# Shifted buffers for the quarters of h, an adding DMA for one branch's low parts, and six raw weight buffers in a three-branch mixer layer

## The chip, the cores and the metric

The kernel runs on one core of one Trainium2 chip. The metric is the device time of one execution in microseconds; of several runs the median is given. TensorE does the matmuls, VectorE (DVE in the rows) and ScalarE (ACT) prepare their operands and finish their results, GpSimd (POOL) does small work, and SyncE (SP) issues the loads. PEld is TensorE's loading of the stationary operand, which overlaps the matmuls.

## The reference, cut to what matters

x has 512 tokens of 1,024 channels, all in float32. One layer is computed:

```python
h = rmsnorm(x, norm_g)
proj = h @ w_in                       # 1024 x 12288
a_u, a_v, a_z, b_p, b_z, c_h, c_b, c_c, c_z, gate_logits = split(proj)
ya = spatial_gating(gelu(a_u), gelu(a_v), ...) * silu(a_z)
yb = multiscale_pool(b_p, pool_w, pool_b, pool_scale) * silu(b_z)
yc = c_b * causal_depthwise_conv(c_c * c_h, conv_w, conv_b) * silu(c_z)
gates = sigmoid(gate_logits)          # three of 1024 channels
merged = gates[0]*(ya @ w_branch_a) + gates[1]*(yb @ w_branch_b) + gates[2]*(yc @ w_branch_c)
out = rmsnorm(x + merged @ w_out)
```

## The kernel before

Each float32 operand of a matmul is split into a high part (rounded to the format that TensorE reads, `F32R`) and a low part (what is left). A product of two operands is then three matmuls: high by high, high by low and low by high (`mm3`, lines 97 to 101). The high part of a weight is a cast on ScalarE and the low part a subtraction on VectorE (`split`, lines 51 to 54).

A weight goes through three pools. `load_raw` (lines 56 to 59) fetches it into one of seven `wraw` buffers of 4 KB per partition, on SP's queue. `load_w` (lines 61 to 66) splits it into one of four `whi` and one of four `wlo` buffers. A buffer is used again as soon as its last reader is through, so SP's queue waits for raw buffers, and ScalarE's casts wait for TensorE to release high parts.

The projections of h are computed in 22 groups of 512 output channels (`group`). A group takes four quarters of its weight, combines them by sums, and makes seven products of 128x256 matmuls (line 435) in place of eight, each with 24 matmuls. h, transposed, is kept as quarters (`b11`, `b21`, `b22`) and as sums of quarters (`t1` to `t4`), each with a high and a low part: 14 buffers of 4 KB per partition from the pool `forms`, made by `form_tile` (lines 170 to 172) under the tags f0 to f6. The seven products stream b11, b21, t2, t1, t3, b22 and t4 in this order. Later the same tags hold the split merged result and the residual.

The branches follow each other: a, b, c. In each, `merge` computes the sigmoid gates in two groups and multiplies the branch's result by its weight: `cols` loads 256 columns in two units of 512 KB with `load_w`, `proj` makes a tile of 128 output channels from 24 matmuls of 512 columns, and `under` multiplies it by the gate and adds it to `merged`. One pair of units serves two tiles. Branch b has four such pairs, two in each half: the first tile of a half is computed by `mix` ahead of the rest of the pending group (b22, t4), the others in `after`. Branch b's pooling, ahead of it, is work for VectorE.

The order of the instructions on each engine is set when the program is built: a planner takes them by their place in the program and by when its own costs say that inputs and buffers are there. Only what stands in `pin` keeps the order of the program (the start, mainly). The same planner deals out buffers and the waits for them.

Of the kernel before, what the change touches and what calls it, by code (L numbers as in the profile page):

```python
# [8 lines left out]
F32 = mybir.dt.float32  # L9
F32R = mybir.dt.float32r  # L10
AF = mybir.ActivationFunctionType
ALU = mybir.AluOpType
PSUM = bass.MemoryType.PSUM

P = 128
# [3 lines left out]
NB = S // P  # L19
HALF = 512  # L20
GC = 256
RMS_EPS = 1e-6
LN_EPS = 1e-5
POOL_WINDOWS = (2, 4, 8, 16)
# [6 lines left out]
def mixers_kernel(ctx, tc, x, norm_g, w_in, sgu_ln_g, sgu_ln_b, sgu_w, sgu_b, pool_w, pool_b, pool_scale,  # L31
                  conv_w, conv_b, w_branch_a, w_branch_b, w_branch_c, w_out, final_g, out):
    nc = tc.nc
# [1 line left out]
    const = ctx.enter_context(tc.tile_pool(name="const", bufs=1))  # L35
    acts = ctx.enter_context(tc.tile_pool(name="acts", bufs=1))
    forms = ctx.enter_context(tc.tile_pool(name="forms", bufs=1))
    wraw = ctx.enter_context(tc.tile_pool(name="wraw", bufs=7))
    wsum = ctx.enter_context(tc.tile_pool(name="wsum", bufs=2))
    whi = ctx.enter_context(tc.tile_pool(name="whi", bufs=4))  # L40
    wlo = ctx.enter_context(tc.tile_pool(name="wlo", bufs=4))
# [9 lines left out]
    def split(hi, lo, src, keep=lambda ins: ins):  # L51

        keep(nc.scalar.copy(out=hi, in_=src))  # L53
        keep(nc.vector.tensor_tensor(out=lo, in0=src, in1=hi.bitcast(F32), op=ALU.subtract))  # L54

    def load_raw(src, shape):
        raw = wraw.tile([P, *shape], F32, tag="wraw", name="wraw")
        nc.sync.dma_start(out=raw, in_=src)
        return raw

    def load_w(src, shape, keep=lambda ins: ins):
        raw = load_raw(src, shape)
        hi = whi.tile([P, *shape], F32R, tag="whi", name="whi")
        lo = wlo.tile([P, *shape], F32R, tag="wlo", name="wlo")
        split(hi, lo, raw, keep)
        return hi, lo

    def cols(w2d, c0):

        v = w2d[:, c0 : c0 + GC].rearrange("(k p) c -> p k c", p=P)  # L70
        units = [load_w(v[:, 4 * h : 4 * h + 4, :], [4, GC]) for h in range(2)]

        def at(k, j):
            hi, lo = units[k // 4]
            return hi[:, k % 4, j * P : (j + 1) * P], lo[:, k % 4, j * P : (j + 1) * P]

        return at

    def halves(w2d, c0, keep=lambda ins: ins, homes=None):

        v = w2d[:, c0 : c0 + HALF].rearrange("(k p) c -> p k c", p=P)
        units = []
        for h in range(4):
            src = v[:, 2 * h : 2 * h + 2, :]
            if homes is None:
                units.append(load_w(src, [2, HALF], keep=keep))
            else:
                split(*homes[h], load_raw(src, [2, HALF]), keep)
                units.append(homes[h])

        def at(k):
            hi, lo = units[k // 2]
            return hi[:, k % 2, :], lo[:, k % 2, :]

        return at
# [73 lines left out]

    def form_tile(name, tag):  # L170

        return tuple(forms.tile([P, 4, GC], F32R, tag=f"{tag}{e}", name=f"{name}{e}") for e in ("h", "l"))


    hq = {(0, 0): form_tile("b11", "f0"), (1, 0): form_tile("b21", "f1"), (1, 1): form_tile("b22", "f2"),
          (0, 1): form_tile("b12", "f6")}

    def h_at(e, k, b):
# [5 lines left out]
    def x_rstd(b, parts=1):  # L184
        n = D // parts
        ms = RMS_EPS
        for i in range(parts):
# [140 lines left out]

    hsum = acts.tile([P, 4, 4, GC], F32, tag="ylo", name="hsum")
    for i, q in enumerate([(0, 0), (0, 1), (1, 1), (1, 0)]):  # L330
# [4 lines left out]
    def sum_form(name, tag, out, in0, in1):  # L335
        nc.vector.tensor_tensor(out=out, in0=in0, in1=in1, op=ALU.subtract)
        moving[name] = form_tile(name, tag)
        split(*moving[name], out)
# [29 lines left out]
    for b in range(NB):  # L368
        v_tile(w, b, 1)
        if b == 0:  # L370
            sbias = const.tile([P, KT, P], F32, tag="pad1", name="sbias")
            for h in range(2):
                ps = bank()
                nc.tensor.matmul(ps, lhsT=ones, rhs=wsT[:, 4 * h : 4 * h + 4, :], start=True, stop=True)
                for g in range(4):
                    t = 4 * h + g
# [20 lines left out]
    def proj(w, j, rhs_hi, rhs_lo, nk=KT):  # L397
        ps = bank()
        for k in range(nk):
            mm3(ps, w(k, j), (rhs_hi[:, k, :], rhs_lo[:, k, :]), k == 0, k == nk - 1)  # L400
        return ps

    def tile512(name):
        return tmp.tile([P, PAD + S], F32, tag="tmp", name=name)[:, 0:S]

    def out_tile(name):

        return outs.tile([P, 2, 2, S], F32, tag="outs", name=name)
# [5 lines left out]

    T1, T2 = slice(0, GC), slice(GC, S)

# [3 lines left out]
    def group(c0, g, ct, use=None):  # L420
        def quarter(kh, nh):
            c = c0 + nh * HALF + g * GC
            return load_raw(w_in[kh * HALF : (kh + 1) * HALF, c : c + GC].rearrange("(k p) c -> p k c", p=P), [4, GC])
# [88 lines left out]
    def act_into(ct, func):  # L512
        def use(src, half, ts):
            nc.scalar.activation(out=ct[:, half, :, ts], in_=src, func=func)
        return use
# [52 lines left out]
    def merge(br, w_branch):  # L568

        state = {}  # L570

        def gates(g):
            state[g] = out_tile("gate")
            yield from group(OFF[f"g{br}"], g, state[g], act_into(state[g], AF.Sigmoid))

        def split_m(ts):
            hi, lo = m_split[ts.start // 2]
            split(hi, lo, merged[:, ts, :])

        def mixes(g):  # L580
            wb = {}

            def mix(t):
                if t % 2 == 0:
                    wb[t // 2] = cols(w_branch, t * P)
                return proj(wb[t // 2], t % 2, y_hi, y_lo)

            def under(t, ps):
                nonlocal merged
                if merged is None:  # L590
                    merged = acts.tile([P, KT, S], F32, tag="big", name="merged")
                gate = state[g][:, t // 4, t % 2]
                if br == 0:
                    nc.vector.tensor_mul(out=merged[:, t, :], in0=ps, in1=gate)
                    return
                pr = tile512("pr")
                nc.vector.tensor_mul(out=pr, in0=ps, in1=gate)
                nc.vector.tensor_add(out=merged[:, t, :], in0=merged[:, t, :], in1=pr)
                if br == 2 and g == 1 and t % 2 == 1:
                    if not m_split:  # L600
                        for kk in range(4):
                            m_split[kk] = tuple(
                                forms.tile([P, 2, S], F32R, tag=f"f{kk}{e}", name=f"m_{e}") for e in ("h", "l"))
                        split_m(slice(0, 2))
                        split_m(slice(4, 6))
                    split_m(slice(t - 1, t + 1))

            first = mix(TILES[g][0])

            def after():  # L610
                under(TILES[g][0], first)
                for t in TILES[g][1:]:
                    under(t, mix(t))

            return after

        for g in range(2):
            items.append(("group", gates(g), None))
            items.append(("other", lambda g=g: mixes(g)))
# [52 lines left out]
    def pool_mm(p):  # L672
        hi, lo = load_w(pool_w[0, p].rearrange("(k p) c -> p k c", p=P), [2, GC])
        w = lambda k, j: (hi[:, k, j * P : (j + 1) * P], lo[:, k, j * P : (j + 1) * P])
        ts = slice(2 * p, 2 * p + 2)
        pss = [proj(w, j, y_hi[:, ts, :], y_lo[:, ts, :], nk=2) for j in range(2)]

        def after():
            for j, ps in enumerate(pss):
                t = 2 * p + j  # L680
                y = tile512("y")
                nc.vector.scalar_tensor_tensor(out=y, in0=ps, scalar=vec(2, t), in1=silu_z[p % 2][:, p // 2, j],  # L682
                                               op0=ALU.add, op1=ALU.mult)
                nc.scalar.mul(out=y_hi[:, t, :], in_=y, mul=vec(3, t))
                nc.vector.scalar_tensor_tensor(out=y_lo[:, t, :], in0=y, scalar=vec(3, t),  # L685
                                               in1=y_hi[:, t, :].bitcast(F32), op0=ALU.mult, op1=ALU.subtract)

        return after
# [75 lines left out]
    for c in range(2):  # L764
        w = halves(w_out, c * HALF)
        cs = slice(c * HALF, (c + 1) * HALF)
        for b in range(NB):
# [9 lines left out]
            if c == 0:  # L777
                nc.vector.tensor_scalar(out=ms0[:, b : b + 1], in0=ssq, scalar1=1.0 / D, scalar2=RMS_EPS,
                                        op0=ALU.mult, op1=ALU.add)
# [38 lines left out]
```

## Time and profile before

| | |
|---|---|
| median of 3 runs | 714.74 us (714.09 to 715.19) |
| the profiled execution | 714.31 us |
| its span in the profile | 712.1 us |
| TensorE's mean granted clock in it | 0.994 |
| read from HBM | 73.96 MB |

The profile shows one execution, in us from the start of its span. A row of the timeline has the start, the duration, the engine (SPq is SyncE's queue), the line, the operation, what it writes and reads, and in brackets how long the engine stood idle before and what ended that. A matmul's shown duration is longer than its step to the next one, since they overlap. L54 is line 54 of the kernel.

### The profile page before, as it was taken

To read this page: it belongs to the slowest core of one execution; us is meant where nothing else is said; L and a number is where in the kernel's file an instruction comes from. 1 tells how busy PE (TensorE), PEld (TensorE's weight loads), DVE (VectorE), ACT (ScalarE), POOL (GpSimd) and SP (SyncE) were. 2 spreads that over 40 slices of the span, in tenths; PEclk is the share of its full clock that TensorE was granted. 3 is DMA by queue.
4 is the path that set the end of the run, shared out by engine and by line. 5 is a ranking of instruction groups with operands and counts; after the bars stand their busy time and mean duration, and the time that the engine had idled before them with its cause. 6 is when DMAs were issued, how large, how long until landed. Compare 5 with 4: busy or idle time off the path is not lost.

```text
span 712.1 us, 11488 instructions
## 1 busy us (share of the span) xinstructions
PE 697.6 (98%) x4838; PEld 650.7 (91%) x4838; DVE 539.2 (76%) x620; ACT 334.6 (47%) x410; POOL 15.0 (2%) x38
## 2 busy tenths in 40 slices
PE   8999999999999999997999999999999999999996
PEld 6779999999898999996989899999999999898884
DVE  6998789795545799999665777798979986646453
ACT  6534556555233456455434334545545464244232
POOL 3001000000000000000000000000000000000001
PEclk9999999999999999999999999999999999999998
DMA  7822323314141313340514213224332334172002
GB/s 281 260 82 60 114 65 119 119 53 157 58 148 60 114 50 106 117 147 2 179 60 151 86 60 120 89 92 138 97 119 93 117 119 144 63 260 95 1 26 93
DMA packets 68536, 76.81 MB, mean 108 GB/s; under 512 B 2492, under 2 KB 61956, under 8 KB 68484
## 3 DMA queue, kind: packets, MB, share of 16 engines
q1 hardware_dynamic: 67892, 75.02, 32.5%
q10 hardware_dynamic: 592, 1.05, 0.4%
q8 instruction: 38, 0.62, 0.4%
q14 instruction: 14, 0.11, 0.1%
HBM read 73.96 MB, written 2.10 MB: 107 GB/s over the span
## 4 chain that ended last, share of the span: by engine, by line
PE 90%; DVE 6%; DMA 1%; issue 1%; ACT 1%; SPq 0%; POOL 0%; POOLq 0%; ACTq 0%; DVEq 0%
PE ps L435 58%; PE ps L99 9%; PE ps L100 9%; PE ps L101 9%; PE ps L259 2%; DVE wlo L54 1%; DMA x_in<-in_x 1%; PE ps L553 1%; DVE win L658 1%; DVE ylo L685 0%; DVE wraw L448 0%; DVE y L682 0%; ACT whi L53 0%; DVE d L661 0%; DVE ylo L54 0%
## 5 line engine op out<-in xcount | busy, mean ns | idle before, releaser
L53 ACT CAST whi<-wraw 128x1024 fp32r<-128x1024 f32 (+1 forms) x168 | 174.5, 1040 | 275.5 <-PE ps L435 171.0
L54 DVE TENSOR_TENSOR wlo<-wraw,whi 128x1024 fp32r<-128x1024 f32 (+1 forms) x168 | 201.6, 1208 | 84.5 <-ACT whi L53 84.1
L99 PE MATMUL ps<-yhi,whi 128*128 128x512 f32 x208 | 81.1, 390 | 0.0
L100 PE MATMUL ps<-ylo,whi 128*128 128x512 f32 x208 | 81.1, 390 | 0.0
L101 PE MATMUL ps<-yhi,wlo 128*128 128x512 f32 x208 | 80.9, 389 | 0.0
L435 PE MATMUL ps<-b21h,wlo 128*128 128x256 f32 x176 | 50.6, 287 | 3.9 <-DVE wlo L54 3.9
L448 DVE TENSOR_TENSOR wraw<-wraw 128x1024 f32<-128x1024 f32 x44 | 53.6, 1219 | 0.4
L435 PE MATMUL ps<-b22h,whi 128*128 128x256 f32 x176 | 51.1, 290 | 0.0
L435 PE MATMUL ps<-b21h,whi 128*128 128x256 f32 x176 | 50.3, 286 | 0.0
L435 PE MATMUL ps<-t1h,whi 128*128 128x256 f32 x176 | 49.9, 284 | 0.4 <-ACT whi L53 0.4
L435 PE MATMUL ps<-b21l,whi 128*128 128x256 f32 x176 | 50.3, 286 | 0.0
L435 PE MATMUL ps<-t2h,whi 128*128 128x256 f32 x176 | 50.1, 285 | 0.0
L435 PE MATMUL ps<-t2h,wlo 128*128 128x256 f32 x176 | 50.0, 284 | 0.0
L435 PE MATMUL ps<-b11h,wlo 128*128 128x256 f32 x176 | 49.9, 284 | 0.1
L435 PE MATMUL ps<-t1h,wlo 128*128 128x256 f32 x176 | 49.8, 283 | 0.0
L435 PE MATMUL ps<-t3h,whi 128*128 128x256 f32 x176 | 49.8, 283 | 0.0
L435 PE MATMUL ps<-t3l,whi 128*128 128x256 f32 x176 | 49.8, 283 | 0.0
L435 PE MATMUL ps<-t3h,wlo 128*128 128x256 f32 x176 | 49.8, 283 | 0.0
L435 PE MATMUL ps<-t4h,wlo 128*128 128x256 f32 x176 | 49.8, 283 | 0.0
L435 PE MATMUL ps<-t4l,whi 128*128 128x256 f32 x176 | 49.8, 283 | 0.0
L435 PE MATMUL ps<-b11l,whi 128*128 128x256 f32 x176 | 49.8, 283 | 0.0
L435 PE MATMUL ps<-t1l,whi 128*128 128x256 f32 x176 | 49.8, 283 | 0.0
(221 smaller groups left out, 1830.6 us busy)
## 6 DMA issues: line engine op xcount, KB each, us to landing
wraw<-in_w_in SPq DMA_DIRECT2D x96, 512.0 KB, 3.7
wraw<-in_w_branch_a SPq DMA_DIRECT2D x8, 512.0 KB
wraw<-in_w_branch_b SPq DMA_DIRECT2D x8, 512.0 KB, 3.5
wraw<-in_w_branch_c SPq DMA_DIRECT2D x8, 512.0 KB, 4.0
wraw<-in_w_out SPq DMA_DIRECT2D x8, 512.0 KB
res<-in_x SPq DMA_DIRECT2D x4, 512.0 KB, 4.9
x_in<-in_x SPq DMA_DIRECT2D x3, 512.0 KB, 10.1
wraw<-in_pool_w SPq DMA_DIRECT2D x4, 256.0 KB, 2.6
```

The costliest lines, as they stand in the source:

```text
L53: keep(nc.scalar.copy(out=hi, in_=src))
L54: keep(nc.vector.tensor_tensor(out=lo, in0=src, in1=hi.bitcast(F32), op=ALU.subtract))
L99: nc.tensor.matmul(ps, lhsT=a[0], rhs=b[0], start=first, stop=False)
L100: nc.tensor.matmul(ps, lhsT=a[0], rhs=b[1], start=False, stop=False)
L101: nc.tensor.matmul(ps, lhsT=a[1], rhs=b[0], start=False, stop=last)
L259: pin(nc.tensor.matmul(vps[b], lhsT=a, rhs=r, start=done[b] == 1, stop=done[b] == 3 * KT))
L435: nc.tensor.matmul(ps[:, j * GC : (j + 1) * GC], lhsT=a[x][:, k, j * P : (j + 1) * P], rhs=moving[b][y][:, k, :], start=first and j == 0 a ...
L448: nc.vector.tensor_tensor(out=out, in0=in0, in1=in1, op=op)
L553: nc.tensor.matmul(mx[:, n * P : (n + 1) * P], lhsT=v_t[:, n, t * P : (t + 1) * P], rhs=wsT[:, t, :], start=True, stop=True)
L658: nc.vector.tensor_add(out=nxt[:, lo:], in0=cur[:, lo:], in1=cur[:, lo - step : PAD + S - step])
```

## The change

The 14 buffers of `form_tile` get a few more elements each, and the data begin `SHIFT[tag + e]` elements of 4 bytes into them, a number that differs between the tags. In branch b (`br == 1`) `load_w` makes the low part in another way: ScalarE copies the raw weight to the high part and writes the negated high part into the low buffer, and a DMA on GpSimd's queue adds the weight from HBM to it. The pool of raw weights has six buffers in place of seven, and the DMA scratch is 2,048 bytes in place of 1,024.

```diff
--- before.py
+++ after.py
@@ -19,6 +19,9 @@
 NB = S // P
 HALF = 512
 GC = 256
+
+SHIFT = {"f0h": 64, "f0l": 64, "f1h": 0, "f1l": 64, "f5h": 112, "f5l": 112, "f3h": 120, "f3l": 56,
+         "f4h": 32, "f4l": 32, "f2h": 16, "f2l": 16, "f6h": 8, "f6l": 8}
 RMS_EPS = 1e-6
 LN_EPS = 1e-5
 POOL_WINDOWS = (2, 4, 8, 16)
@@ -35,7 +38,7 @@
     const = ctx.enter_context(tc.tile_pool(name="const", bufs=1))
     acts = ctx.enter_context(tc.tile_pool(name="acts", bufs=1))
     forms = ctx.enter_context(tc.tile_pool(name="forms", bufs=1))
-    wraw = ctx.enter_context(tc.tile_pool(name="wraw", bufs=7))
+    wraw = ctx.enter_context(tc.tile_pool(name="wraw", bufs=6))
     wsum = ctx.enter_context(tc.tile_pool(name="wsum", bufs=2))
     whi = ctx.enter_context(tc.tile_pool(name="whi", bufs=4))
     wlo = ctx.enter_context(tc.tile_pool(name="wlo", bufs=4))
@@ -62,8 +65,15 @@
         raw = load_raw(src, shape)
         hi = whi.tile([P, *shape], F32R, tag="whi", name="whi")
         lo = wlo.tile([P, *shape], F32R, tag="wlo", name="wlo")
-        split(hi, lo, raw, keep)
+        if by_dma:
+            nc.scalar.copy(out=hi, in_=raw)
+            nc.scalar.mul(out=lo, in_=hi.bitcast(F32), mul=-1.0)
+            nc.gpsimd.dma_start(out=lo, in_=src, accum_op=ALU.add)
+        else:
+            split(hi, lo, raw, keep)
         return hi, lo
+
+    by_dma = False
 
     def cols(w2d, c0):
 
@@ -169,7 +179,12 @@
 
     def form_tile(name, tag):
 
-        return tuple(forms.tile([P, 4, GC], F32R, tag=f"{tag}{e}", name=f"{name}{e}") for e in ("h", "l"))
+        parts = []
+        for e in ("h", "l"):
+            at = SHIFT[tag + e]
+            t = forms.tile([P, 4 * GC + at], F32R, tag=f"{tag}{e}", name=f"{name}{e}")
+            parts.append(t[:, at:].rearrange("p (k t) -> p k t", k=4))
+        return tuple(parts)
 
 
     hq = {(0, 0): form_tile("b11", "f0"), (1, 0): form_tile("b21", "f1"), (1, 1): form_tile("b22", "f2"),
@@ -605,13 +620,19 @@
                         split_m(slice(4, 6))
                     split_m(slice(t - 1, t + 1))
 
+            nonlocal by_dma
+            by_dma = br == 1
             first = mix(TILES[g][0])
 
             def after():
                 under(TILES[g][0], first)
+                nonlocal by_dma
                 for t in TILES[g][1:]:
+                    by_dma = br == 1
                     under(t, mix(t))
-
+                by_dma = False
+
+            by_dma = False
             return after
 
         for g in range(2):
@@ -801,7 +822,7 @@
     import concourse.bacc as bacc
     from concourse.bass_utils import run_bass_kernel_spmd
 
-    nc = bacc.Bacc("TRN2", target_bir_lowering=False, num_devices=1, dynamic_dma_scratch_size=1024)
+    nc = bacc.Bacc("TRN2", target_bir_lowering=False, num_devices=1, dynamic_dma_scratch_size=2048)
     arrays, args = {}, {}
     for name in _INS:
         a = np.ascontiguousarray(inputs[name])
```

## Rows read from the trace of the kernel before

**Rows 1.** The page, first part: busy time and its share of the span.
```profile
PE 697.6 (98%) x4838; PEld 650.7 (91%) x4838; DVE 539.2 (76%) x620; ACT 334.6 (47%) x410; POOL 15.0 (2%) x38
```

**Rows 2.** Windows: length; busy us of PE, PEld, DVE, ACT, POOL; granted clock; DMA.
```profile
300.00:328.00 28.00, 27.95 (x210) 26.65 (x209) 27.97 (x47) 16.05 (x24) 0.00 (x0) 1.00 0.36 114
328.40:332.20 3.80, 0.00 (x0) 0.00 (x0) 3.54 (x6) 1.91 (x3) 0.00 (x0) 0.94 0.00 0
331.80:335.10 3.30, 2.88 (x13) 2.88 (x14) 3.27 (x4) 0.05 (x1) 0.00 (x0) 0.50 0.00 0
345.90:420.00 74.10, 74.10 (x449) 66.53 (x448) 46.27 (x49) 27.86 (x31) 0.00 (x0) 1.00 0.31 98
```

**Rows 3.** Timeline of VectorE and TensorE at the hole.
```profile
330.95 1.22 DVE L54 TENSOR_TENSOR wlo<-wraw,whi 128x1024 fp32r<-128x1024 f32 x1
...
332.22 0.58 PE L435 MATMUL ps<-b21h,wlo 128*128 128x256 f32 x1 [3.88 <-DVE wlo L54]
```

**Rows 4.** Timeline of TensorE, a product of 256-column matmuls.
```profile
421.44 0.28 PE L435 MATMUL ps<-t2h,wlo 128*128 128x256 f32 x1
421.56 0.28 PE L435 MATMUL ps<-t2h,whi 128*128 128x256 f32 x1
```

**Rows 5.** Timeline of ScalarE: the casts of the eight units of w_branch_b.
```profile
338.10 1.05 ACT L53 CAST whi<-wraw 128x1024 fp32r<-128x1024 f32 x1
340.48 1.05 ACT L53 CAST whi<-wraw 128x1024 fp32r<-128x1024 f32 x1 [1.32 <-PE ps L435]
...
354.38 1.05 ACT L53 CAST whi<-wraw 128x1024 fp32r<-128x1024 f32 x1 [4.81 <-PE ps L435]
...
357.26 1.05 ACT L53 CAST whi<-wraw 128x1024 fp32r<-128x1024 f32 x1 [0.87 <-ACT gate L514]
...
379.31 1.05 ACT L53 CAST whi<-wraw 128x1024 fp32r<-128x1024 f32 x1 [1.29 <-PE ps L435]
382.19 1.05 ACT L53 CAST whi<-wraw 128x1024 fp32r<-128x1024 f32 x1 [1.83 <-PE ps L435]
...
396.34 1.05 ACT L53 CAST whi<-wraw 128x1024 fp32r<-128x1024 f32 x1 [4.81 <-PE ps L435]
...
399.22 1.05 ACT L53 CAST whi<-wraw 128x1024 fp32r<-128x1024 f32 x1 [0.87 <-ACT gate L514]
```

**Rows 6.** Timeline of TensorE: first matmuls that read those units' low parts.
```profile
346.38 0.39 PE L101 MATMUL ps<-yhi,wlo 128*128 128x512 f32 x1
...
349.12 0.39 PE L101 MATMUL ps<-yhi,wlo 128*128 128x512 f32 x1
...
363.06 0.39 PE L101 MATMUL ps<-yhi,wlo 128*128 128x512 f32 x1
...
388.34 0.39 PE L101 MATMUL ps<-yhi,wlo 128*128 128x512 f32 x1
...
405.02 0.39 PE L101 MATMUL ps<-yhi,wlo 128*128 128x512 f32 x1
```

**Rows 7.** The page, DMA: a queue (packets, MB, share); issues (size, us to landing).
```profile
q1 hardware_dynamic: 67892, 75.02, 32.5%
...
wraw<-in_w_in SPq DMA_DIRECT2D x96, 512.0 KB, 3.7
...
wraw<-in_w_branch_b SPq DMA_DIRECT2D x8, 512.0 KB, 3.5
...
x_in<-in_x SPq DMA_DIRECT2D x3, 512.0 KB, 10.1
```

**Rows 8.** Timeline of SyncE, VectorE and ScalarE in the steady stretch of branch c.
```profile
415.08 0.37 SPq L58 DMA_DIRECT2D wraw<-in_w_in  x1
...
421.24 0.37 SPq L58 DMA_DIRECT2D wraw<-in_w_in  x1
...
418.85 1.22 DVE L448 TENSOR_TENSOR s<-wraw 128x1024 f32<-128x1024 f32 x1 [0.65 <-DMA wraw<-in_w_in]
...
432.84 1.05 ACT L53 CAST whi<-wraw 128x1024 fp32r<-128x1024 f32 x1 [1.39 <-issue]
```

## The prediction

> **What bounds the kernel now.** I read the page's busy times first: TensorE is busy for 98% of the span and VectorE for 76% [rows 1]. The reader should see that little but matmul time can be won. The windows come next, over the one stretch where TensorE stands still [rows 2]: from 300 to 328 us VectorE is busy for all but 0.03 us of 28, then TensorE does nothing for the 3.8 us from 328.4, and its granted clock is 0.50, the 1.2 GHz level, for the 3.3 us after 331.8. The timeline names the cause [rows 3]: the low part of a weight was made on VectorE only at 330.95, and the matmul behind it waited 3.88 us. Elsewhere matmuls follow each other at a fixed step: 0.12 us at 256 columns [rows 4]. At 2.4 GHz 256 columns are 0.107 us, so some 13 ns of each step are not columns. So the kernel is bound by TensorE, with one hole of about 5.5 us (3.8 idle, and half of the 3.3 us at 1.2 GHz, 1.7) that VectorE makes.
>
> **Part 1, the offsets.** They add no instruction and no byte. The 14 buffers start at other addresses, all shifts multiples of 32 bytes (8 elements of 4). What could change is the step of the 22 x 7 x 24 = 3,696 matmuls that stream these buffers. The kernel before has all 14 at the same place modulo 4 KB, so no row shows another place. Upper bound of the gain: all 13 ns go, 3,696 x 13 = 48 us. Bound of the loss, from the same row mirrored: 13 ns more, +48 us. I take zero: within a quarter the four slices and the two weight halves start 1,024 and 512 bytes apart, and the step is 0.12 us from one to the next all the same [rows 4].
>
> **Part 2, the adding DMA.** In branch b alone (8 of the 132 loads of weights), the subtraction on VectorE goes, and a negated copy on ScalarE and a second fetch of the weight by a DMA that adds come in its place. Removed: 8 x 1.22 us on VectorE [rows 3]. They stand at 340 us and later, behind the hole [rows 2], so by themselves they can't fill it. Added: 8 negations on ScalarE, each like the cast, 1.05 us [rows 5]; ScalarE has gaps of 0.87 to 4.81 us beside those casts, so they fit. Added on GpSimd: 8 DMA issues, which wait for the negation; GpSimd has nothing else until the last stage (no busy time in the windows [rows 2]), so nobody is queued behind them there. Added on the DMA engines: 8 x 512 KB.
>
> What counts is the time from the end of the negation to the first matmul that reads the low part, the third one of each tile (line 101). There are four pairs of loads. First of each pair: the casts end at 339.15, 355.43, 380.36 and 397.39 us; with 1.05 for the negation the DMA can start at 340.20, 356.48, 381.41 and 398.44 [rows 5]. The matmuls that need it start at 346.38, 363.06, 388.34 and 405.02 [rows 6]. Slack: 6.2, 6.6, 6.9 and 6.6 us. Second of each pair: starts at 342.58, 359.36, 384.29 and 401.32, needed 2.74 us (twelve matmuls) after the first [rows 6]; slack 6.5, 6.4, 6.8 and 6.4 us. The slack is about the same each time because a buffer for the high part only comes free when TensorE has finished with the product four places earlier.
>
> The DMA itself is in no row. From below: a plain load of these bytes from this tensor lands 3.5 us after its issue, 3.7 for w_in. From above: the early loads of x, which stood behind others, took 10.1 [rows 7]. An adding DMA has to read the destination as well as the source; as two loads one after the other, that is 2 x 3.7 = 7.4 us. I take 7.4, which lies near the middle. The first units are then late by 1.2, 0.8, 0.5 and 0.8, together 3.3 us. The second ones share the engines with the first: 75.02 MB took 32.5% of the 16 engines' 712 us [rows 7], so 512 KB take 1.6 us of all of them and with two reads 3.2 us. The second starts 2.4 us after the first in pair one and 2.9 in the others, so it loses another 0.8 and three times 0.3 us. Its waits, after the first one's wait has moved TensorE, are 0.5, 0.5, 0.4 and 0.5, together 1.9. Sum of part 2: 5.2 us. All of it is on the path: behind a waiting matmul stands every later one. Gaps of about 1 us are far below the 3.8 us that stood before the slow clock [rows 2], so I add nothing for the clock.
>
> The Trainium skill speaks for less. Its page "DMA: Bandwidth & Descriptors" (Anatomy of one DMA, the GpSimd path) gives 2.0 us plus the bytes over 436 GB/s, which for 512 KB is an estimate of 3.2 us. "Collectives: The Full Stack" (The bandwidth ceiling) says that an add in the DMA costs two source reads and not the adding itself. By both together the DMA would take about 4.4 us, no matmul would wait, and the sum would be zero. No run here shows either yet.
>
> **Part 3, six raw buffers instead of seven.** Each load waits for one more release on SP's queue. In a group of the steady stretch, the load issued at 415.08 would go out at the next release, 421.24, and land 3.7 us later, at 424.9; the sum on VectorE that now starts at 418.85 waits for it [rows 8]. After it come two more operations of 1.22 us, so the operand is ready at 428.6. The cast that reads it runs at 432.84 [rows 8], for a product still further off: 4.2 us of margin, cost zero. If VectorE's order were kept as it is, other low parts would stand behind that late sum; their lead is about two products of 24 x 0.12 = 2.9 us, against a delay of 6.1, so 0.3 to 0.4 us a group and, over the 20 groups that follow another, at most 8 us. The order is the planner's, made anew with six buffers, so I keep zero and leave the 8 to the range. From below nothing: fewer buffers release nothing sooner. SP's queue holds only loads there.
>
> **Sum.** The profiled execution took 714.31 us; with 5.2 it is 719.5. That execution was 0.43 under the median of the runs shown, so the forecast is 719.9.
>
> **Rivals.** *Hidden* (0.22): the DMA lands within 6.2 us, and nothing waits: 714.7 us. For it: the plain load's 3.7 leaves 2.5 us for the second read. Against: another queue, and each pair overlaps on the engines. The two pages of the Trainium skill above speak for this case.
>
> *A slow queue* (0.17): either the DMA takes the upper bound of 10.1 us, the first units wait 3.9, 3.5, 3.2 and 3.5 and the second ones some 2 in all, +16, 731 us; or the second DMA starts only when the first has landed. Then the second lands 14.8 us after the first could start, 4.7 us late, each pair loses 5.5, and the gaps are long enough for the slow clock (1.7 each) [rows 2]: 4 x 7.2 = 29, 743 us. Nothing in this trace shows that queue at work.
>
> *The hole closes* (0.14), the other side: with six buffers and eight fewer operations the planner orders VectorE's work anew, and the late low part [rows 3] no longer stands behind the others. It decides if that subtraction starts before 328 instead of at 330.95. Price: the 5.5 us of the hole, 709.2, if the DMA is hidden too. Against: the removed operations come later than the hole, and VectorE's work ahead of it is all still there.
>
> *The offsets matter* (0.10), also faster: two reads on the way to TensorE that now start at the same place modulo 4 KB stop disturbing each other. It decides once the step of any of the seven products falls below 0.12 us; half of the 13 ns would be 24 us, 691. Against it: the even step at every slice [rows 4].
>
> **How the numbers follow.** The forecast has 0.37. About 0.2% (1.4 us) is what a measurement of this kernel can tell from no change. Faster: 0.14 + 0.10 = 0.24. Within it: 0.22. Slower: 0.37 + 0.17 = 0.54. The range goes from 709, the closed hole, to 733, just above the DMA's upper bound; it leaves out the offsets' 0.10 and about half of the slow queue, 0.08, and holds the 8 us of part 3. A loss from the offsets has no chance of its own: no row hints at one.
>
> **What would show it.** Right: matmuls of line 101 in the four tiles that open a pair with a wait of about 1 us that ends on a DMA; GpSimd's queue with 8 issues and a landing of 7 to 8 us; 4 MB more read; the step at 0.12 us in all seven products; the hole near 328 us as before. Wrong: a landing under 6 us with no wait (hidden), one DMA starting only when the last has ended (slow queue), a step under 0.12 us in some product (offsets), or no hole (planner).

## The result and the profile after

The changed kernel takes 743.97 us (741.88 to 745.72), the kernel before 714.70 in the runs beside it: the ratio is 1.0409, with a 95% interval of 1.0376 to 1.0441. The change costs 29.3 us.

The page of the kernel after, its busy times (they answer to [rows 1]), its DMA queues and issues (to [rows 7]) and the costliest group with a new wait. The last number of an issue's line is the median time from the issue to the landing, when all the data are there:

```profile
PE 705.6 (95%) x4838; PEld 651.4 (88%) x4838; DVE 530.1 (72%) x612; ACT 342.6 (46%) x418; POOL 25.7 (3%) x46
...
q1 hardware_dynamic: 67892, 75.02, 31.5%
q0 software_dynamic: 4224, 4.19, 3.7%
...
L111 PE MATMUL ps<-yhi,wlo 128*128 128x512 f32 x208 | 85.7, 412 | 18.4 <-DMA wlo<-in_w_branch_b 18.4
...
wlo<-in_w_branch_b POOLq DMA_DIRECT2D x8, 512.0 KB, 6.9
```

VectorE has 9.1 us less to do and TensorE as many matmuls as before, but the third matmul of `mm3` (line 101 before, 111 now) stands idle for 18.4 us, all of it behind the adding DMA. GpSimd's timeline in the kernel after shows the first four of its eight issues:

```profile
340.44 1.45 POOL L71 DMA_DIRECT2D wlo<-in_w_branch_b  x1 [194.75 <-PE ps L450]
350.93 1.32 POOL L71 DMA_DIRECT2D wlo<-in_w_branch_b  x1 [9.04 <-issue]
365.25 1.29 POOL L71 DMA_DIRECT2D wlo<-in_w_branch_b  x1 [13.00 <-ACT wlo L70]
373.15 1.31 POOL L71 DMA_DIRECT2D wlo<-in_w_branch_b  x1 [6.61 <-DVE wlo L57]
```

TensorE's timeline in the kernel after shows the eight waits, in brackets:

```profile
350.71 0.79 PE L111 MATMUL ps<-yhi,wlo 128*128 128x512 f32 x1 [4.42 <-DMA wlo<-in_w_branch_b]
356.60 0.50 PE L111 MATMUL ps<-yhi,wlo 128*128 128x512 f32 x1 [0.40 <-DMA wlo<-in_w_branch_b]
372.88 0.50 PE L111 MATMUL ps<-yhi,wlo 128*128 128x512 f32 x1 [2.15 <-DMA wlo<-in_w_branch_b]
378.92 0.50 PE L111 MATMUL ps<-yhi,wlo 128*128 128x512 f32 x1 [1.42 <-DMA wlo<-in_w_branch_b]
404.11 0.79 PE L111 MATMUL ps<-yhi,wlo 128*128 128x512 f32 x1 [2.49 <-DMA wlo<-in_w_branch_b]
410.61 0.57 PE L111 MATMUL ps<-yhi,wlo 128*128 128x512 f32 x1 [1.92 <-DMA wlo<-in_w_branch_b]
428.80 0.50 PE L111 MATMUL ps<-yhi,wlo 128*128 128x512 f32 x1 [2.45 <-DMA wlo<-in_w_branch_b]
434.98 0.79 PE L111 MATMUL ps<-yhi,wlo 128*128 128x512 f32 x1 [3.16 <-DMA wlo<-in_w_branch_b]
```

Look at the second issue. It goes out at 350.93, and TensorE, which waits for the first DMA, goes on at 350.71. So GpSimd issues the second DMA of the pair only when the first has landed. In the second pair it is the same: 373.15 after 372.88, and in the third and fourth too (404.38 after 404.11, 429.06 after 428.80). The brackets of GpSimd's rows name other releasers there, or none; a releaser is inferred, and a run with more room for the queue settles it below. ScalarE's timeline in the kernel after says that the second DMA's own input was there long before: the second negation of pair one (starts 341.77) ends at 342.83, that of pair two (starts 366.22) at 367.26.

```profile
341.77 1.06 ACT L70 ACTIVATE wlo<-whi 128x1024 fp32r<-128x1024 f32 x1
...
361.94 1.05 ACT L69 CAST whi<-wraw 128x1024 fp32r<-128x1024 f32 x1 [12.62 <-PE ps L450]
362.89 1.06 ACT L529 ACTIVATE gate<-gate 128x1024 f32<-128x1024 f32 x1
363.85 1.04 ACT L70 ACTIVATE wlo<-whi 128x1024 fp32r<-128x1024 f32 x1
...
366.22 1.04 ACT L70 ACTIVATE wlo<-whi 128x1024 fp32r<-128x1024 f32 x1
```

The windows of the kernel after (columns as in [rows 2]) give the clock, and the whole of branch b's merge in the last row:

```profile
345.90:420.00 74.10, 61.30 (x334) 52.24 (x333) 25.91 (x28) 24.62 (x28) 6.51 (x5) 0.88 0.52 119
349.40:356.30 6.90, 5.49 (x12) 3.79 (x12) 2.45 (x2) 0.00 (x0) 1.32 (x1) 0.51 0.96 232
373.30:376.80 3.50, 3.50 (x10) 2.72 (x9) 1.11 (x1) 0.00 (x0) 1.16 (x1) 0.51 0.48 69
338.00:460.00 122.00, 103.59 (x608) 90.49 (x606) 50.77 (x54) 44.00 (x50) 10.56 (x8) 0.92 0.49 117
```

In the 74.1 us where TensorE did 449 matmuls before [rows 2], it now does 334, at a mean clock of 0.88. Behind five of the eight waits (4.42, 2.15, 2.49, 1.92 and 3.16 us) stands a stretch at 1.2 GHz; two are shown, the others begin at 404.1, 410.9 and 434.8 and last 3.4 us each. That is 20.5 us, of which some 1.8 are idle (first columns), so about 9.3 us are lost to the clock. Idle time and clock, 18.4 + 9.3, make 27.7 us. The other two parts of the change together take 0.7 us off (714.08 for 714.82 in the run with the offsets alone, below), so the DMA costs some 30 us, and about 2.3 of them are in neither term and stay unassigned.

The hole [rows 3] is still there, a little earlier and as long (TensorE's timeline after):

```profile
332.09 0.39 PE L450 MATMUL ps<-b21h,wlo 128*128 128x256 f32 x1 [3.87 <-DVE wlo L57]
```

### The profile page after: what moved, and what is told of

It is laid out like the page before. It is cut to its first block, busy times and chain, and to the rows that moved or that the text cites. A ratio compares the mean times of both kernels' runs of the same rounds, so it can differ in the third digit from the quotient of the medians.

```text
span 740.7 us, 11514 instructions
## 1 busy us (share of the span) xinstructions
PE 705.6 (95%) x4838; PEld 651.4 (88%) x4838; DVE 530.1 (72%) x612; ACT 342.6 (46%) x418; POOL 25.7 (3%) x46
## 3 DMA queue, kind: packets, MB, share of 16 engines
q0 software_dynamic: 4224, 4.19, 3.7%
q10 hardware_dynamic: 592, 1.05, 0.4%
## 4 chain that ended last, share of the span: by engine, by line
PE 76%; issue 8%; DVE 8%; DMA 5%; ACT 2%; POOL 0%; SPq 0%; POOLq 0%; ACTq 0%; DVEq 0%
PE ps L450 47%; PE ps L111 8%; PE ps L109 8%; PE ps L110 8%; DMA wlo<-in_w_branch_b 2%; DVE wlo L57 2%; PE ps L274 2%; DVE wraw L463 2%; DMA wraw<-in_w_in 1%; DMA x_in<-in_x 1%; PE ps L568 1%; DVE cc L761 1%; ACT whi L56 1%; PE ps L224 0%; DVE ylo L706 0%
## 5 line engine op out<-in xcount | busy, mean ns | idle before, releaser
L56 ACT CAST whi<-wraw 128x1024 fp32r<-128x1024 f32 (+1 forms) x160 | 166.4, 1041 | 265.7 <-PE ps L450 151.3
L57 DVE TENSOR_TENSOR wlo<-wraw,whi 128x1024 fp32r<-128x1024 f32 (+1 forms) x160 | 191.9, 1206 | 80.0 <-ACT whi L56 79.6
L111 PE MATMUL ps<-yhi,wlo 128*128 128x512 f32 x208 | 85.7, 412 | 18.4 <-DMA wlo<-in_w_branch_b 18.4
L109 PE MATMUL ps<-yhi,whi 128*128 128x512 f32 x208 | 84.5, 406 | 0.0
L110 PE MATMUL ps<-ylo,whi 128*128 128x512 f32 x208 | 84.4, 406 | 0.0
L111 PEld LDWEIGHTS ps<-yhi,wlo 128*128 128x128 f32 x208 | 41.2, 198 | 30.8 <-DMA wlo<-in_w_branch_b 22.1
L450 PE MATMUL ps<-t2l,whi 128*128 128x256 f32 x176 | 50.1, 284 | 0.0
L450 PE MATMUL ps<-b11h,whi 128*128 128x256 f32 x176 | 49.7, 282 | 0.0
L450 PE MATMUL ps<-b22h,wlo 128*128 128x256 f32 x176 | 49.5, 281 | 0.0
L450 PE MATMUL ps<-t4h,whi 128*128 128x256 f32 x176 | 49.5, 281 | 0.0
```

Of the source, the lines that this page charges most:

```text
L109: nc.tensor.matmul(ps, lhsT=a[0], rhs=b[0], start=first, stop=False)
L110: nc.tensor.matmul(ps, lhsT=a[0], rhs=b[1], start=False, stop=False)
L111: nc.tensor.matmul(ps, lhsT=a[1], rhs=b[0], start=False, stop=last)
L450: nc.tensor.matmul(ps[:, j * GC : (j + 1) * GC], lhsT=a[x][:, k, j * P : (j + 1) * P], rhs=moving[b][y][:, k, :], start=first and j == 0 a ...
```

## The experiments

Ten kernels, each beside runs of the kernel before (714.8 to 715.0 us). Three take the change apart, three ask why the DMA is late, four follow the offsets.

**Six raw buffers alone.** The kernel before with:

```diff
-    wraw = ctx.enter_context(tc.tile_pool(name="wraw", bufs=7))
+    wraw = ctx.enter_context(tc.tile_pool(name="wraw", bufs=6))
```

> The kernel before with six raw weight buffers, nothing else. Theory (the loss lies in the adding DMAs, waiting in one line): 714.7 us, within 0.2% of before, since a raw buffer is refilled well before its split. Rival (the loads from memory now start late, and TensorE waits for them in all groups): 720 us or more, with new TensorE waits outside branch b's merge.

Measured: 716.59 us, ratio 1.0025 (1.0015 to 1.0034). Neither the theory nor the rival: a small loss, 1.8 us. VectorE's waits over the whole span show it (us in total, times, longest), first in the kernel before:

```profile
DVE s L448 <- DMA wraw<-in_w_in: 10.7, 10, 2.7
```

With six raw buffers:

```profile
DVE s L448 <- DMA wraw<-in_w_in: 27.5, 17, 4.2
```

TensorE's timeline with six raw buffers has a wait that the kernel before has not:

```profile
326.65 0.39 PE L435 MATMUL ps<-b11h,wlo 128*128 128x256 f32 x1 [0.98 <-DVE wlo L54]
```

The sums on VectorE wait for late loads 17 times instead of 10. Most of that is in VectorE's spare time; near 326 us, where it has none, a low part comes 1 us late. That the late loads are behind this one is argued from these counts; no row links them.

**The offsets alone.** The kernel after with `by_dma` always false and the scratch of before.

```diff
-            by_dma = br == 1
+            by_dma = False
             first = mix(TILES[g][0])
...
-                    by_dma = br == 1
+                    by_dma = False
```

> The offsets with six raw buffers, no adding DMA. Theory (the changed kernel's step of 118.5 ns for 119.9, over some 3,630 matmuls of 256 columns, is the offsets' own): 5 us off, 0.5 back on the merges' 512-column matmuls, so about 710 us. Rival (the shorter step comes from something else in the changed kernel, as the lower clock around the waits): 714.7 us and a step of 119.9 ns.

Measured: 714.08 us, 2.5 us under six raw buffers alone; to the kernel before the ratio is 0.9988 (0.9978 to 0.9997). The mean distance between the starts of neighbouring matmuls of a product at full clock is 118.5 ns over the seven products (119.9 before), as in the kernel after. So the step is the offsets' own. The gain is half of what was expected: 1.4 ns on 3,696 matmuls are 5.2 us, 0.5 goes back on the 512-column matmuls that read the split merged result (229 ns for 227), and 1.5 us more of TensorE's time goes into waits, most of them for VectorE.

**The adding DMA alone.** The kernel after with zero offsets.

```diff
+SHIFT = {f"f{i}{e}": 0 for i in range(7) for e in "hl"}
```

> The adding DMA and its queue memory of 2048 with six raw buffers, offsets all zero. Theory: the eight adding DMAs cost all of the loss and the offsets hid some 4.5 us of it: 748 to 750 us, eight TensorE waits of 20 us in sum and five stretches at half clock in branch b's merge. Rival (offsets and DMA together make the loss, by slower writes to shifted tiles): about 730 us.

Measured: 747.88 us, ratio 1.0462 (1.0444 to 1.0479), 31.3 us over six raw buffers alone. TensorE's waits from 338 to 460 us (in total, times, longest) and the window over the same stretch:

```profile
PE ps L110 <- DMA wlo<-in_w_branch_b: 22.4, 8, 5.8
```

```profile
338.00:460.00 122.00, 99.55 (x578) 86.83 (x578) 48.30 (x52) 42.70 (x48) 10.56 (x8) 0.92 0.49 112
```

The loss is the adding DMA's, and again each second issue on GpSimd follows the landing of the first. Two theories for its queue were open: the second DMA waits for the first itself, or for room in the queue's memory.

**More room for the queue.** The same, with:

```diff
-    nc = bacc.Bacc("TRN2", target_bir_lowering=False, num_devices=1, dynamic_dma_scratch_size=2048)
+    nc = bacc.Bacc("TRN2", target_bir_lowering=False, num_devices=1, dynamic_dma_scratch_size=4096)
```

> As the run with the adding DMA alone, with the memory of GpSimd's DMA queue at 4096 for 2048. If the second DMA of a pair waits for room in that memory: it issues within 2 us of the end of its negation and both land within some 10 us of it, so the waits of the second units go or shrink and the time falls to 735 us or less. If it waits for the first DMA itself, whatever the room: the same 748 to 750 us as with 2048.

Measured: 733.48 us, ratio 1.0254 (1.0235 to 1.0274): 14.4 us come back. GpSimd's timeline (first pair) in this kernel, then TensorE's waits, the window over the merge, and the landing times of the eight DMAs, each from its view:

```profile
341.75 1.45 POOL L70 DMA_DIRECT2D wlo<-in_w_branch_b  x1 [195.63 <-PE ps L449]
344.45 1.29 POOL L70 DMA_DIRECT2D wlo<-in_w_branch_b  x1 [1.25 <-ACT wlo L69]
```

```profile
PE ps L110 <- DMA wlo<-in_w_branch_b: 11.9, 5, 4.5
```

```profile
338.00:460.00 122.00, 109.61 (x694) 98.84 (x694) 59.13 (x61) 49.59 (x56) 10.49 (x8) 0.96 0.52 125
```

```profile
DMA to landing us min/median/max: 7.6/8.4/12.2
```

The second issue is now released by its own negation, 2.7 us after the first. So with 2,048 bytes the queue had room for one of these DMAs, and waiting for the first was worth nearly half of the loss. The larger half, 16.9 us over six raw buffers alone, stays: four first units and one second wait, since each DMA takes 7.6 us or more.

**A plain copy in place of the adding one.** The room stays at 4,096. This kernel leaves out the addition, so branch b's low parts hold the raw weights.

```diff
-            nc.gpsimd.dma_start(out=lo, in_=src, accum_op=ALU.add)
+            nc.gpsimd.dma_start(out=lo, in_=src.bitcast(F32R))
```

> As the run with queue memory 4096, but the GpSimd DMA copies the raw weight over the negated tile and adds nothing, so branch b's low parts hold the wrong values; everything else is the same. If the adding (a second read per packet) makes the DMA slow: packets fall from 104 ns to about half, the landing of an undisturbed DMA by 1.5 to 2 us, the first units' waits from 2.2 to 2.5 us to under 1 us, and the time to 722 to 727 us. If the queue itself makes it slow (writing its descriptors, its start): landing within 0.5 us of the adding run, and 731 to 734 us again.

Measured: 719.24 us, ratio 1.0064 (1.0049 to 1.0079). Of this kernel, the queue on the page, the landing times, the one wait that is left, and the window, each from its view:

```profile
q0 software_dynamic: 4224, 4.19, 2.6%
```

```profile
DMA to landing us min/median/max: 4.0/4.8/8.3
```

```profile
PE ps L110 <- DMA wlo<-in_w_branch_b: 2.3, 1, 2.3
```

```profile
338.00:460.00 122.00, 119.66 (x819) 111.34 (x819) 71.66 (x73) 56.56 (x64) 6.14 (x8) 1.00 0.48 138
```

A share of 2.6% of 16 engines over 717 us is 298 us, or 73 ns for each of the 4,096 packets of 1 KB; adding, it was 107 ns (3.7% of 740.7). Less than half the time went, but with it the median landing falls from 8.4 to 4.8 us, under the slack, and the clock stays at 1.00. So adding in place of copying, with its longer issue on GpSimd (1.29 us for 0.74), costs 14.2 us, most of the 16.9 that the larger room had left.

**The same DMA with more slack.** Adding again, room 4,096, and branch b's matmuls in another order:

```diff
...
+                        for part_ in range(2):
+                            for j in range(2):
+                                for k in range(KT):
+                                    hi, lo = wb[t // 2](k, j)
+                                    if part_ == 0:
+                                        nc.tensor.matmul(pss[j], lhsT=hi, rhs=y_hi[:, k, :], start=k == 0, stop=False)
+                                        nc.tensor.matmul(pss[j], lhsT=hi, rhs=y_lo[:, k, :], start=False, stop=False)
+                                    else:
+                                        nc.tensor.matmul(pss[j], lhsT=lo, rhs=y_hi[:, k, :], start=False, stop=k == KT - 1)
...
```

> As the run with queue memory 4096 (adding DMA, offsets zero), with one thing moved: in branch b each pair of output tiles does its 32 matmuls on high parts of the weight first and its 16 on low parts after them. Each low part is then needed 5 to 6.8 us later (7.3 us into the pair for 0.45). Theory (what costs is a landing 2 to 5 us later than the slack, and the half clock behind it): no TensorE wait on a low part is left, no stretch at half clock but the hole's at 328 us, and the time is that of six raw buffers alone, 716.6 us, within 2 us. Rival (the loads of memory themselves, 4 MB more, or the negations on ScalarE slow the merge): over 722 us with the waits gone.

Measured: 718.68 us, ratio 1.0053 (1.0038 to 1.0068), 2.1 us over six raw buffers alone. The landing times, TensorE's waits and the window of this kernel:

```profile
DMA to landing us min/median/max: 5.8/8.7/12.7
```

```profile
PE ps L612 <- DMA wlo<-in_w_branch_b: 1.8, 1, 1.8
```

```profile
338.00:460.00 122.00, 119.64 (x817) 110.84 (x817) 70.99 (x74) 57.20 (x64) 10.55 (x8) 1.00 0.56 138
```

The DMAs land no sooner (8.7 us), and of the eight units only one still waits; its 1.8 us, behind the landing of 12.7, are nearly all of the rest. So the loss was lateness against the slack and the clock behind it, not the bytes. In this kernel the DMA also wins nothing: VectorE is busy 12 us less in this window than with six raw buffers alone (70.99 for 83.26), and TensorE gains nothing by it. With six raw buffers alone:

```profile
338.00:460.00 122.00, 121.71 (x840) 113.69 (x839) 83.26 (x84) 50.40 (x58) 0.00 (x0) 1.00 0.35 108
```

**Which offsets, and why.** In the kernel before, the 14 buffers and the weight buffers all begin at the same place modulo 256 bytes. In the kernel after, the weight buffers still do (the shifts add up to 2,816 bytes, eleven times 256), and each shift pushes all buffers behind it. The products then differ as this table shows (places of high and low part in bytes modulo 256, counted from the weights' place; the step is the mean distance of starts at full clock):

| product | high, low | step, ns |
|---|---|---|
| all seven, before | 0, 0 | 119.9 |
| b11, b21 | 0, 0 | 119.6, 119.9 |
| t2 | 64, 0 | 118.8 |
| t4 | 160, 192 | 118.5 |
| b22 | 64, 128 | 117.9 |
| t1 | 160, 128 | 117.7 |
| t3 | 0, 128 | 117.3 |

My first two kernels looked at the two parts alone, not yet at the weights. To the kernel with the offsets alone they make one edit each. Kernel (a) shifts every buffer but the first by 32 elements:

```diff
+SHIFT = {'f0h': 0, 'f0l': 32, 'f1h': 32, 'f1l': 32, 'f2h': 32, 'f2l': 32, 'f6h': 32, 'f6l': 32, 'f3h': 32, 'f3l': 32, 'f4h': 32, 'f4l': 32, 'f5h': 32, 'f5l': 32}
```

Kernel (b) shifts the first alone, and with it all that lies behind:

```diff
+SHIFT = {'f0h': 32, 'f0l': 0, 'f1h': 0, 'f1l': 0, 'f2h': 0, 'f2l': 0, 'f6h': 0, 'f6l': 0, 'f3h': 0, 'f3l': 0, 'f4h': 0, 'f4l': 0, 'f5h': 0, 'f5l': 0}
```

> Offsets alone, six raw buffers, no adding DMA: each quarter's low part begins 128 bytes further, modulo 256, than its high part, for all seven products; the high parts stay at their place modulo 256. If the step depends on where the two parts lie to each other: about 117.3 ns in all seven products (what the one product with this distance has), 9.5 us less matmul time than with six raw buffers alone, 716.6, and 708 to 711 us as some of it goes to waits for VectorE. If it depends on the absolute place: between 117.3 and 119.9 ns, and differently for the parts.

> Offsets alone, six raw buffers, no adding DMA: all 14 buffers begin 128 bytes further than before, so that the two parts lie to each other as before. If the step depends on where the two parts lie to each other: 119.9 ns in all products and 716.6 us, as with six raw buffers alone. If it depends on the absolute place modulo 256: below 119 ns in all seven, and 708 to 713 us.

Measured: (a) 721.04 us, 119.8 ns; (b) 720.38 us, 119.9 ns in all products. Both theories fall: (a) has t3's distance between the parts and none of its gain, (b) has another place and the old step. And both are slower than six raw buffers alone, mainly by the merges' 512-column matmuls, whose data had not moved: 233 and 232 ns for 227. What had moved by 128 bytes was their weights, which lie behind the shifted buffers. So the place to look at is that of the data against the weights: (0, 0) in (b), where both moved; (128, 0) in (a). The next kernel leaves the 14 buffers where they were and moves the weights, with all else that lies behind those buffers: no shifts, and 128 bytes left free behind the last of them.

```diff
-            t = forms.tile([P, 4 * GC + at], F32R, tag=f"{tag}{e}", name=f"{name}{e}")
+            end = 32 if tag + e == "f5l" else 0
+            t = forms.tile([P, 4 * GC + at + end], F32R, tag=f"{tag}{e}", name=f"{name}{e}")
...
```

> Six raw buffers, no adding DMA; the 14 buffers at the very addresses of the kernel before, and everything behind them (the weight buffers among them) 128 bytes further. If the step depends on the place of the streamed data alone: 120.0 ns in all seven products, 716.6 us. If it depends on where the data lie to the weights, modulo 256: another step in all seven products, over 122 ns, as the merges' 512-column matmuls went from 227 to 233 ns when the weights moved by 128 and their data did not; that is 7 us or more, 724 us or over.

Measured: 718.99 us (two runs, 717.97 and 720.02), ratio 1.0057 (1.0038 to 1.0075). The data of the seven products are where they were, and their step is 118.8 ns in place of 119.9; the 512-column matmuls take 233 ns. So what the seven products save, some 4 us, is about what the 512-column matmuls lose, and the profile's granted clock is lower besides (0.990, for 0.995 with six raw buffers alone). I had the sign wrong for the seven products, but the data's own place cannot do this. Nor can the weights' own place: in (b) the weights lie as here, the data moved with them, and the step is the old one. The last kernel gives all seven products t3's arrangement (0, 128), with the high parts in a row, 128 bytes, then the low parts, and so room for seven raw buffers:

```diff
...
+    for e in "hl":
+        for tag in ("f0", "f1", "f2", "f6", "f3", "f4", "f5"):
+            n = 4 * GC + SHIFT[tag + e] + (32 if tag + e == "f5l" else 0)
+            forms.tile([P, n], F32R, tag=f"{tag}{e}", name="place")
...
```

The shift is 32 for the first low part, `f0l`, and zero for the others.

> Offsets alone with seven raw buffers, no adding DMA: the seven high parts stand one behind the other, at the weights' own place modulo 256, then 128 bytes are left free, then the seven low parts; 256 bytes in all, so that the seventh raw buffer fits. If the place relative to the weights decides: all seven products take the 117.3 ns of the one product that had this arrangement in the changed kernel (t3), 9.5 us less matmul time, of which VectorE's waits give back a part: 707 to 712 us, the fastest so far. If the distance between the parts decides: about 119.8 ns, as where only that distance was set, and 714 us or more.

Measured: 709.96 us (709.83 to 710.51), ratio 0.9932 (0.9918 to 0.9945): 4.9 us faster than before. The seven products have 117.7 to 117.9 ns. The groups of instructions, with shapes kept apart, show the same in a matmul's mean duration (ns, ahead of the second bar). First the kernel before:

```profile
L435 PE MATMUL ps<-b11h,whi 128*128 128x256 f32 x176 | 49.8, 283 | 0.0
L99 PE MATMUL ps<-yhi,whi 128*128 128x512 f32 x208 | 81.1, 390 | 0.0
```

Then kernel (b):

```profile
L449 PE MATMUL ps<-b11h,whi 128*128 128x256 f32 x176 | 49.8, 283 | 0.0
L108 PE MATMUL ps<-yhi,whi 128*128 128x512 f32 x208 | 82.0, 394 | 0.0
```

Then the kernel with the weights moved:

```profile
L450 PE MATMUL ps<-b11h,whi 128*128 128x256 f32 x176 | 49.5, 281 | 0.0
L108 PE MATMUL ps<-yhi,whi 128*128 128x512 f32 x208 | 82.1, 395 | 0.0
```

And the last one:

```profile
L455 PE MATMUL ps<-b11h,whi 128*128 128x256 f32 x176 | 49.3, 280 | 0.0
L108 PE MATMUL ps<-yhi,whi 128*128 128x512 f32 x208 | 81.0, 389 | 0.0
```

The sum: 2.15 ns on 3,696 matmuls are 7.9 us; 0.7 goes back on the split merged result (232 ns for 227 in 128 matmuls); the other 2.3 are in part longer waits for VectorE and ScalarE, and the rest is not taken apart. What the two reads share that makes the place matter is not shown, nor whether 256 bytes is the true period: it was only argued from the table.

## Why the prediction was wrong

**What bounds the kernel**: right. The hole is still there (3.87 us for 3.88), and what TensorE waited for the DMA, 18.4 us, shows in the time together with the clock's loss behind it.

**The work that part 2 removes and adds**: right. Eight subtractions less on VectorE, eight negations of 1.05 us, 4.19 MB on a new queue, the waits where I looked for them.

**"The second starts 2.4 us after the first ... and 2.9 in the others, so it loses another 0.8 and three times 0.3 us"**: this is the step that failed. The second started when the first had landed, 10.5 us after the first in pair one, since the queue's memory held one such DMA. I read the larger scratch in the diff as a detail and costed it at nothing. With double the room the DMAs overlap as I took them to, and 14.4 us return. With that room, and the 3.9 us that the offsets give beside the DMA (747.88 to 743.97), I estimate 730 us for the change, inside the range.

**The slack, "they fit"**: mis-sized for pairs two and four. Between cast and negation stands a gate's operation (L529, 362.89); the negation ended at 364.89, 1.9 us behind the cast's end and not 1.05. The gate operation beside the casts was in [rows 5].

**The landing of 7.4 us**: near the middle of what came (5.6 to 10.2, median 6.9), but the first units, with a slack of 6.2 to 6.9 by my working, could not use a median: theirs were 10.2, 7.6, 8.9 and 7.8 us. First units waited 11.5 us for my 3.3, second ones 6.9 for my 1.9. Two pages of the Trainium skill spoke for less: by "DMA: Bandwidth & Descriptors" (Anatomy of one DMA) the estimate was 3.2 us for a plain one and, with the second source read of "Collectives: The Full Stack" (The bandwidth ceiling), 4.4 for an adding one. Measured at their best: 4.0 and 5.6. That adding costs more agrees in its direction, 107 ns a packet for 73; no trace here shows that a second read is the reason.

**"I add nothing for the clock"**: wrong, as six of the eight waits were not about 1 us but 1.9 to 4.4. It cost some 9 us.

**Part 1, zero**: off by 2.5 us on the gain's side. The step did not depend on the slice, as [rows 4] said; slices are 1,024 bytes apart, and the offsets that mattered are below 256. The row could not speak to them. The rival *offsets matter* had the right place and too high a price: 5 us of matmul time, not 24.

**Part 3, zero**: off by 1.8 us, inside its bound of 8. The late loads came on VectorE's sums as described; the margin of 4.2 us that I read in branch c is not there at 326 us.

**The rivals**: *a slow queue*, in its second form, is what happened: 743 us by my working, 743.97 measured, and I gave both of its forms 0.17 together and left the 743 out of the range. Its sum was right by parts that were not: I had 4.7 us of waiting in each second unit and 0.8 in each first one, and the first ones waited more than the second. *Hidden* is what 5 to 7 us more slack would make of the DMA, but for one wait. *The hole closes* fell: the hole stayed, with VectorE busy 27.77 of the 28 us ahead of it (27.97 before).

## What to carry to other kernels

A DMA that replaces an engine's operation has to land within the slack each time, not at the median: list the slack of every instance, with every operation that its engine may put in front, and set it against the slowest landing. Ask of a new queue how many transfers its memory holds at once; if it is one, the second of two starts when the first has landed. And when matmuls bind, try where the streamed operand begins against the stationary one: 128 bytes took 2 ns off a step of 120 in one arrangement, and put 5 to 6 ns on one of 227 in another.

## What the runs showed of the hardware that I had not expected

The clock fell to 1.2 GHz behind waits of TensorE as short as 1.92 us (at 410.9) and did not behind one of 2.45 (at 428.80), in the same profile. With the larger room it did not fall behind waits of 2.23 and 2.09 us either. A wait's length alone does not tell.

The stretch at 1.2 GHz behind the hole was 3.4 us long in some profiles and 6.8 in others, with the same hole: the windows of six raw buffers alone, and of the kernel (b).

```profile
334.50:337.90 3.40, 3.40 (x17) 3.17 (x16) 3.33 (x4) 1.45 (x2) 0.00 (x0) 0.50 0.00 0
```

```profile
334.10:340.90 6.80, 6.08 (x28) 6.08 (x29) 6.73 (x8) 3.39 (x5) 0.00 (x0) 0.50 0.00 0
```

At half the clock 3.4 us more are some 1.7 us of work lost, between two profiles that no edit explains, about the size of the smaller effects here: the kernels with the plain copy, (a), (b) and the moved weights all had the long one.

A place of 128 bytes against the weights makes the step of 256 columns shorter (118.8 for 119.9 ns) and that of 512 columns longer (233 for 227). Why the first DMA of a pair takes 2 to 4.5 us more to land than the second stays open; loads on SP's queue run beside some of the first ones, and not beside all.
